# Two four-byte constants in one tile: moving the SBUF tiles of a TensorE-bound kernel by 32 bytes

## The chip, the cores and the metric

The kernel runs on one core of a Trainium2 chip. The metric is the device time of one execution in microseconds. Engines are called TensorE (PE; its weight loads are listed as PEld), VectorE (DVE), ScalarE (ACT), GpSimd (POOL) and SyncE (SP, which issues the DMA transfers here).

## The reference

A two-layer encoder trunk over 256 frames of width 2048, all in float32. Layer 0 mixes in time with an RWKV-7 recurrence of 32 heads, layer 1 with a forgetting attention of 16 heads over shared keys and values. Each is followed by an MLP of width 8192. In short:

```python
x = x + rwkv7_time_mix(rms_norm(x, mix_norm[0]), ...)          # r, k, v projections, decay, gates, recurrence, w_o
x = x + squared_relu_mlp(rms_norm(x, ffn_norm[0]), w_up[0], w_down[0])
k, v, cum_log_f = shared_kv_forget(x, kv_norm, w_kvf, b_f)
x = x + forgetting_attention(rms_norm(x, mix_norm[1]), w_q, w_o, k, v, cum_log_f)
x = x + squared_relu_mlp(rms_norm(x, ffn_norm[1]), w_up[1], w_down[1])
return rms_norm(x, final_norm)

def rms_norm(x, gain):      # RMS_EPS = 1e-6; the recurrence's own norm uses LNX_EPS = 64e-5
    return x * rsqrt(mean(x * x) + RMS_EPS) * gain
def squared_relu_mlp(h, w_up, w_down):
    return square(relu(h @ w_up)) @ w_down
```

## The kernel before

The stream x lies transposed in SBUF, 128 partitions by 16 blocks of 256 frames (`xT`). A projection's weights are streamed from HBM. Each weight and each operand is split into a high part in float32r (fp32r, a float32 that TensorE takes at one column a cycle) and a low part, the rest; a product is the sum of three: high by high, high weight by low operand, low weight by high operand. The operands are kept in two tiles of 32 KB per partition, `opA` and `opB`: for each of the 16 blocks 256 columns of the high part, then 256 of the low.

`load_split` (L192 to L210) fetches a piece of raw weights into `wr`, ScalarE rounds it into `wh` (L204; VectorE at L202 for some), and VectorE or GpSimd takes the rest into `wl` (L206). From there:

- `gemm_steps` (L218) issues three matmuls of 256 columns for each 128x128 block of weights (L212 to L214 in `mm3`). The RWKV stage, the attention's projections and its output use it: 28 groups of 512 output columns in all.
- `gemm_wide` (L240) is the MLP's. For each block of weights it issues one matmul of 512 columns, the high weight over high and low operand together (L254), and one of 256 columns, the low weight over the high operand (L256). This pair is run 4096 times: 64 groups x 16 x 4.
- The values' projection (L933 to L935) turns the roles around: the weights move, 512 columns, over blocks of `opB`. 16 forget-gate columns are projected with `mm3` into `zp`, where the stationary block has 16 columns.
- The gates' projections (L472, L507, L562), the transposes and the attention's own products (L951 to L978) are in plain fp32, each of which is issued as two instructions.

The order of the two streams of the RWKV stage is a table of start and end times (`PLAN_A`, `PLAN_B`); the rest is in program order, with transfers all on SP's queue.

Tiles are laid out in SBUF one after another, each rounded up to 32 bytes per partition. The pool of constants comes first. It begins at byte 16512, a multiple of 64, and holds `vec` (1216 bytes), `k32` (3328), `k16` (1024), `bf` (32), `ones` (512), `eps_r` (32), `eps_l` (32), `negv` (128), `WC` (256) and `onesr` (512), together 7072. The pools of raw and split weights, of the operands, and then of each stage follow from byte 23584. Nearly all larger tiles are multiples of 64 bytes, so that they all lie 32 bytes off a multiple of 64; those behind an odd number of smaller tiles in their own pool (`kk2` and `bk` of the RWKV stage; `qT`, `csb`, `lg`, `pt` and `o` of the attention) lie on one.

`eps_r` is the bias of the norms' logarithm (`Norm.ln`, L326, and L426), `eps_l` that of the recurrence's norm (L819). Each is set by a memset on GpSimd.

Of the kernel before, what the change touches and what calls it, by code (L numbers as in the profile page):

```python
# [10 lines left out]
F32 = mybir.dt.float32  # L11
# [7 lines left out]
P = 128  # L19
# [100 lines left out]
def trunk_kernel(ctx: ExitStack, tc: tile.TileContext, xin, vecs, bfv, c32, c16, w_rkv, w1, w2, a1, a2, g1, g2,  # L120
# [11 lines left out]
    cpool = ctx.enter_context(tc.tile_pool(name="const", bufs=1))  # L132
# [23 lines left out]
    dma(bf, bfv)  # L156
    ones = cpool.tile([P, P], F32, name="ones")
    G.memset(ones, 1.0)
    eps_r = cpool.tile([P, 1], F32, name="eps_r")
    G.memset(eps_r, RMS_EPS)  # L160
    eps_l = cpool.tile([P, 1], F32, name="eps_l")
    G.memset(eps_l, LN_EPS)
    negv = cpool.tile([P, 2 * KT], F32, name="negv")

# [909 lines left out]
def build(nc, arrays):  # L1074
    args = []
    for name, v in arrays.items():
        args.append(nc.dram_tensor(f"in_{name}_dram", v.shape, mybir.dt.from_np(v.dtype), kind="ExternalInput").ap())
    args.append(nc.dram_tensor("out_0_dram", (D, T), F32, kind="ExternalOutput").ap())
    with tile.TileContext(nc) as tc:  # L1079
        trunk_kernel(tc, *args)  # L1080
# [11 lines left out]
```

## Time and profile before

| | before |
|---|---|
| median of 3 runs | 2562.56 us (2562.14, 2562.56 and 2572.66) |
| the profiled execution | 2563.87 us |
| its span, first to last instruction | 2562.1 us |
| TensorE busy | 2474.4 us, 97% |
| VectorE, ScalarE, GpSimd busy | 1620.4, 1272.2, 526.2 us |
| mean granted TensorE clock | 0.993 |
| read from HBM, written | 445.70 MB, 24.13 MB |

The profile is of one execution. Busy times of an engine are unions over its instructions. A matmul's duration overlaps that of the next, because matmuls are pipelined; how fast they follow one another is read from their starts, or from their number in a stretch without idle time. The granted clock (PEclk) of 1.00 is 2.4 GHz, of 0.50 1.2 GHz.

### The profile page before, as it was taken

To read this page: it belongs to the slowest core of one execution; us is meant where nothing else is said; L and a number is where in the kernel's file an instruction comes from. 1 tells how busy PE (TensorE), PEld (TensorE's weight loads), DVE (VectorE), ACT (ScalarE), POOL (GpSimd) and SP (SyncE) were. 2 spreads that over 40 slices of the span, in tenths; PEclk is the share of its full clock that TensorE was granted. 3 is DMA by queue.
4 is the path that set the end of the run, shared out by engine and by line. 5 is a ranking of instruction groups with operands and counts; after the bars stand their busy time and mean duration, and the time that the engine had idled before them with its cause. 6 is when DMAs were issued, how large, how long until landed. Compare 5 with 4: busy or idle time off the path is not lost. (4 is left out here: it accounts for less than half of the span.)

```text
span 2562.1 us, 47095 instructions
## 1 busy us (share of the span) xinstructions
PE 2474.4 (97%) x19102; PEld 2208.3 (86%) x19102; DVE 1620.4 (63%) x2266; ACT 1272.2 (50%) x2098; POOL 526.2 (21%) x428
## 2 busy tenths in 40 slices
PE   6889999999999999999999999999999999999997
PEld 4889988888888888888888898999988888888886
DVE  8987557776755555555556655677555555555555
ACT  3655435454555454454455544455454454554454
POOL 5444324332311211111112100010011112111112
PEclk9999999999999999999999999999999999999998
DMA  4668856555765555555556366546455555556553
GB/s 149 199 201 246 249 180 189 161 166 159 237 202 189 182 181 197 182 189 188 181 181 197 97 183 196 181 158 198 149 190 184 194 187 191 183 195 194 186 195 116
DMA packets 279641, 472.88 MB, mean 185 GB/s; under 512 B 52464, under 2 KB 62976, under 8 KB 279424
## 3 DMA queue, kind: packets, MB, share of 16 engines
q1 hardware_dynamic: 279424, 469.89, 57.9%
q8 instruction: 149, 2.44, 0.4%
q14 instruction: 68, 0.56, 0.1%
HBM read 445.70 MB, written 24.13 MB: 183 GB/s over the span
## 5 line engine op out<-in xcount | busy, mean ns | idle before, releaser
L206 DVE TENSOR_TENSOR wl<-wr,wh 128x1024 fp32r<-128x1024 f32 (+1 forms) x960 | 965.9, 1010 | 740.9 <-ACT wh L204 735.7
L204 ACT CAST wh<-wr 128x1024 fp32r<-128x1024 f32 (+1 forms) x969 | 815.8, 846 | 909.7 <-PE mmw L254 595.0
L254 PE MATMUL mmw<-opB,wh 128*128 128x512 f32 x2048 | 717.4, 397 | 4.9 <-DVE xT L850 4.9
L254 PE MATMUL mmw<-opA,wh 128*128 128x512 f32 x2048 | 718.0, 397 | 0.2 <-ACT wh L204 0.2
L256 PE MATMUL mmw<-opA,wl 128*128 128x256 f32 x2048 | 572.5, 280 | 0.9 <-DVE wl L206 0.9
L256 PE MATMUL mmw<-opB,wl 128*128 128x256 f32 x2048 | 571.7, 279 | 0.0
L254 PEld LDWEIGHTS mmw<-opB,wh 128*128 128x128 f32 x2048 | 384.9, 188 | 97.4 <-DVE xT L850 5.1
L254 PEld LDWEIGHTS mmw<-opA,wh 128*128 128x128 f32 x2048 | 384.9, 188 | 93.0 <-ACT wh L204 0.5
L256 PEld LDWEIGHTS mmw<-opA,wl 128*128 128x128 f32 x2048 | 386.5, 189 | 1.4 <-DVE wl L206 1.3
L256 PEld LDWEIGHTS mmw<-opB,wl 128*128 128x128 f32 x2048 | 386.4, 189 | 0.2
L212 PE MATMUL mm<-opB,wh 128*128 128x256 f32 x1024 | 304.0, 297 | 1.2 <-DVE wh L202 1.2
L214 PE MATMUL mm<-opB,wl 128*128 128x256 f32 x1024 | 294.7, 288 | 7.0 <-DVE wl L206 4.8
L213 PE MATMUL mm<-opB,wh 128*128 128x256 f32 x1024 | 294.6, 288 | 3.9 <-DVE opB L343 3.8
L366 POOL TENSOR_TENSOR xT<-xT,mt 128x512 f32<-128x512 f32 x60 | 128.8, 2147 | 533.8 <-DVE mt L363 533.8
L212 PE MATMUL mm<-opA,wh 128*128 128x256 f32 x768 | 227.7, 297 | 0.0
L214 PE MATMUL mm<-opA,wl 128*128 128x256 f32 x768 | 218.5, 285 | 2.7 <-POOL wl L206 1.5
L213 PE MATMUL mm<-opA,wh 128*128 128x256 f32 x768 | 218.8, 285 | 0.0
L353 POOL TENSOR_TENSOR ms<-mt 128x512 f32<-128x512 f32 x64 | 81.1, 1267 | 636.5 <-ACT mt L351 636.5
L214 PEld LDWEIGHTS mm<-opB,wl 128*128 128x128 f32 x1024 | 198.4, 194 | 9.2 <-DVE wl L206 5.6
L213 PEld LDWEIGHTS mm<-opB,wh 128*128 128x128 f32 x1024 | 198.4, 194 | 7.5 <-DVE opB L343 5.7
L212 PEld LDWEIGHTS mm<-opB,wh 128*128 128x128 f32 x1024 | 198.2, 194 | 5.4 <-DVE wh L202 1.4
L214 PEld LDWEIGHTS mm<-opA,wl 128*128 128x128 f32 x768 | 147.5, 192 | 3.7 <-POOL wl L206 1.7
(252 smaller groups left out, 2711.0 us busy)
## 6 DMA issues: line engine op xcount, KB each, us to landing
wr<-in_mlp_w_up_dram SPq DMA_DIRECT2D x128, 1024.0 KB, 5.4
wr<-in_mlp_w_down_dram SPq DMA_DIRECT2D x128, 1024.0 KB, 5.0
wr<-in_w_rkv_dram SPq DMA_DIRECT2D x96, 512.0 KB, 4.7
wr<-in_w_kvf_dram SPq DMA_DIRECT2D x64, 512.0 KB, 3.7
wr<-in_w_o_dram SPq DMA_DIRECT2D x32, 512.0 KB, 4.0
wr<-in_fox_w_q_dram SPq DMA_DIRECT2D x32, 512.0 KB, 3.8
wr<-in_fox_w_o_dram SPq DMA_DIRECT2D x32, 512.0 KB, 4.0
s_bk<-bk SPq DMA_DIRECT2D x8, 512.0 KB, 3.0
```

Of the source, the lines that this page charges most:

```text
L204: nc.scalar.copy(h, raw[:, k:k + per, :])
L206: (G if share["l"] and c % share["l"] == 0 else V).tensor_tensor(lo, raw[:, k:k + per, :], h.bitcast(F32), op=ALU.subtract)
L212: mm(ps, wh, xh, start=first and bank_first, stop=False, skip_group_check=True)
L213: mm(ps, wh, xl, start=False, stop=False, skip_group_check=True)
L214: mm(ps, wl, xh, start=False, stop=last, skip_group_check=True)
L254: mm(ps[m], h[:, m * P:(m + 1) * P], x[:, k].rearrange("p h t -> p (h t)"), start=k == 0, stop=False, skip_group_check=True)
L256: mm(ps[m][:, 0:T], lo[:, m * P:(m + 1) * P], x[:, k, 0, :], start=False, stop=k == KT - 1, skip_group_check=True)
L353: G.tensor_tensor(s, t, t, op=ALU.mult)
L366: (V if end and g == 3 else G).tensor_tensor(xs, xs, t, op=ALU.add)
```

## The change

The two constants become the two columns of one tile of eight bytes, which is rounded up to 32 bytes as each of them was. What lies behind it in SBUF begins 32 bytes lower: `wr` at 23552 in place of 23584, `opA` at 60416 in place of 60448, and so on. The tiles that lay 32 bytes off a multiple of 64 now lie on one; `kk2`, `bk`, `qT`, `csb`, `lg`, `pt` and `o`, which lay on one, now lie 32 bytes off. `vec`, `k32`, `k16`, `bf` and `ones` stay. The distances between moved tiles stay as they are. Each engine has the same instructions in the same order, and the two memsets are there as before.

```diff
     ones = cpool.tile([P, P], F32, name="ones")
     G.memset(ones, 1.0)
-    eps_r = cpool.tile([P, 1], F32, name="eps_r")
+    eps = cpool.tile([P, 2], F32, name="eps")
+    eps_r, eps_l = eps[:, 0:1], eps[:, 1:2]
     G.memset(eps_r, RMS_EPS)
-    eps_l = cpool.tile([P, 1], F32, name="eps_l")
     G.memset(eps_l, LN_EPS)
     negv = cpool.tile([P, 2 * KT], F32, name="negv")
```

## Rows read from the trace of the kernel before

**Rows 1.** The page: busy us of the engines, and GB/s moved in 40 slices.

```profile
PE 2474.4 (97%) x19102; PEld 2208.3 (86%) x19102; DVE 1620.4 (63%) x2266; ACT 1272.2 (50%) x2098; POOL 526.2 (21%) x428
GB/s 149 199 201 246 249 180 189 161 166 159 237 202 189 182 181 197 182 189 188 181 181 197 97 183 196 181 158 198 149 190 184 194 187 191 183 195 194 186 195 116
```

**Rows 2.** Stretches by stage: from:to, length, busy us (instructions) per engine, clock, DMA.

```profile
36.00:350.00 314.00, 290.05 (x2741) 268.50 (x2739) 244.99 (x376) 167.75 (x332) 137.94 (x120) 0.99 0.70 216
350.00:694.00 344.00, 322.48 (x5127) 289.83 (x5125) 237.78 (x432) 175.10 (x381) 106.31 (x99) 0.99 0.58 174
694.00:1414.00 720.00, 718.44 (x4069) 623.87 (x4070) 424.70 (x469) 349.49 (x475) 118.69 (x71) 1.00 0.58 188
1414.00:1832.00 418.00, 412.16 (x2995) 390.87 (x2994) 267.61 (x497) 210.56 (x408) 29.59 (x40) 1.00 0.54 169
1832.00:2543.00 711.00, 711.00 (x4100) 621.33 (x4099) 407.62 (x445) 349.48 (x467) 114.39 (x69) 1.00 0.57 184
```

**Rows 3.** Waits: who waited for whom, us in total, times, longest.

```profile
ACT wh L204 <- PE mmw L254: 595.0, 359, 1.9
...
ACT wh L204 <- DMA wr<-in_w_rkv_dram: 15.9, 6, 3.8
...
PE hps L425 <- DVE part L424: 11.0, 3, 9.4
PE lps L472 <- POOL xs L451: 10.3, 9, 4.7
...
ACT wh L204 <- DMA wr<-in_mlp_w_up_dram: 2.3, 1, 2.3
```

**Rows 4.** Stretches of PE alone, the MLP of layers 0 and 1.

```profile
726.00:1404.00 678.00, 678.00 (x3838) 1.00 0.58 186
...
1879.00:2521.00 642.00, 642.00 (x3706) 1.00 0.59 190
```

**Rows 5.** Timeline of PE: start us, us; weights of 16 columns, first and 34th.

```profile
1429.15 0.28 PE L212 MATMUL zp<-opB,wh 128*16 128x256 f32 x1
...
1432.89 0.28 PE L212 MATMUL zp<-opB,wh 128*16 128x256 f32 x1
```

**Rows 6.** Timeline of PE: the values' projection, first and 43rd of a run.

```profile
1605.15 0.39 PE L934 MATMUL mmv<-wh,opB 128*128 128x512 f32 x1
...
1614.67 0.39 PE L934 MATMUL mmv<-wh,opB 128*128 128x512 f32 x1
```

**Rows 7.** Timeline of PE: triples of the keys' projection, first and 15th matmul.

```profile
1439.79 0.28 PE L214 MATMUL mm<-opB,wl 128*128 128x256 f32 x1
...
1441.47 0.28 PE L213 MATMUL mm<-opB,wh 128*128 128x256 f32 x1
```

**Rows 8.** Timeline of PE: plain fp32, eight matmuls merged, and the first of them.

```profile
242.19 1.89 PE L507 MATMUL mmg<-gh,wr 128*128 128x256 f32 x8
...
242.19 0.38 PE L507 MATMUL mmg<-gh,wr 128*128 128x256 f32 x1
```

**Rows 9.** Timeline of POOL and ACT: the first memset and the first reader.

```profile
0.88 0.10 POOL L160 MEMSET eps_r<- 128x1 f32 x1
...
15.55 0.47 ACT L426 ACTIVATE gh<-hps,eps_r 128x256 f32<-128x256 f32 x1 [5.04 <-PE hps L425]
```

**Rows 10.** Groups by line and shape: busy us, mean ns, idle before.

```profile
L342 ACT CAST opB<-o 128x256 fp32r<-128x256 f32 x16 | 6.5, 407 | 15.5 <-DVE o L980 15.5
L342 ACT CAST opA<-y 128x256 fp32r<-128x256 f32 x16 | 6.5, 406 | 7.1 <-POOL y L183 6.7
L989 DVE TENSOR_TENSOR qT<-mm,nrq 128x512 f32<-128x512 f32 x8 | 5.4, 683 | 0.0
L916 DVE TENSOR_TENSOR kT<-mm,nr 128x512 f32<-128x512 f32 x8 | 5.1, 682 | 0.0
```

**Rows 11.** Timeline of PE: layer 1's first group, first and 61st matmul of L254.

```profile
1833.06 0.40 PE L254 MATMUL mmw<-opA,wh 128*128 128x512 f32 x1
...
1854.26 0.40 PE L254 MATMUL mmw<-opA,wh 128*128 128x512 f32 x1
```

## The prediction

> **What bounds the kernel now.** I read the busy table first, then the stages, then the steps of TensorE's stream. TensorE (PE) is busy 97% of the span, VectorE (DVE) 63%, ScalarE (ACT) 50% [rows 1]. By stages [rows 2]: both MLP stages (694 to 1414 us and 1832 to 2543 us, 56% of the span) leave PE 1.6 us idle in 1431 us. The attention stage (1414 to 1832) leaves 6, the RWKV stage (36 to 694) 45 in 658. Outside of these lie 36 us of head and 19 of tail. In the MLP the other engines are under 60% busy, and ACT's longest wait there is for PE (595.0 us, for weight buffers to come free), while its waits for weight loads come to 2.3 us for the MLP and 15.9 for the RWKV stage [rows 3]. So the pace at which PE takes one matmul after another sets the time, and whatever doesn't touch that pace is worth a few us.
>
> That pace is above what the columns ask for. I turn each step into cycles at 2.4 GHz, since the granted clock reads 1.00 in the stretches used [rows 4].
> - fp32r, 256 columns, weights of only 16 columns: 33 steps from 1429.15 to 1432.89 us, 113.3 ns = 272 cycles [rows 5]: 16 over the 256 columns.
> - fp32r, 512 columns: 42 steps from 1605.15 to 1614.67 us, 226.7 ns = 544 cycles [rows 6]: 32 over.
> - the usual fp32r triple (L212 to L214), 256 columns and weights of 128: 14 steps from 1439.79 to 1441.47 us, 120.0 ns = 288 cycles [rows 7]: 32 over.
> - the MLP pair (512 and 256 columns, two weight loads): 678 us for 3838 matmuls, 353.3 ns a pair = 848 cycles in layer 0; 642 us for 3706, 346.5 ns = 832 in layer 1 [rows 4]. Over the 768 columns: 80 and 64.
> - plain fp32 (L507), where a column takes two cycles, so that the read runs at half the rate: eight in 1.89 us, each 0.38 long, so 7 steps of 216 ns = 518 cycles for 512 [rows 8]: 6 over.
>
> The excess comes in pieces of 16 cycles per 256 columns, and 16 cycles is the time of 16 columns, 64 bytes per partition. A run of 1024 bytes touches 16 pieces of 64 bytes if it begins on a multiple of 64, and 17 if it begins 32 bytes past one; 17 pieces are 272 cycles. Every fp32r operand here begins 32 past one: the tiles from the raw weights on start at byte 23584 = 368 x 64 + 32. For the 512 columns this needs two reads of 1024 bytes (one of 2048 would be 33 pieces, 528 cycles), so the fit isn't perfect. The fp32 row reads tiles 32 off as well (gh, wr) and shows none of it, as half the rate would leave room to spare. And the weight loads, 512 bytes each (9 pieces for 8), appear as 8 cycles each in layer 1 (832 - 816 = 16 for two) and 16 in layer 0 and in the triples. I take this as the likeliest reading, not as shown: no fp32r operand in this trace lies on a multiple of 64, so nothing separates it from a cost that fp32r always has.
>
> **The change part by part.** *Code:* no instruction is added, removed or moved on any engine. The two memsets on GpSimd (POOL) stay, the first one 0.10 us long at 0.88 us, and their first reader runs at 15.55 us [rows 9], so that the norm's reader now depends on both of them costs nothing; without that lead it would be one memset, 0.10 us.
>
> *Addresses:* everything past the constants moves down by 32 bytes. opA, opB, xT, wr, wh, wl, mt, ms, the inverse's and the recurrence's tiles go from 32 off to a multiple of 64. A few go the other way: kk2, bk, qT, csb, lg, pt and o.
>
> *VectorE, ScalarE:* the same write of 128x512 takes 683 ns into qT (on 64 now) and 682 into kT (32 off); the same cast takes 407 ns from o (on 64) and 406 from y (32 off) [rows 10]. Nothing either way.
>
> *The FoX tiles that go off 64:* their matmuls are fp32 (32 each at L951, L952, L977 and L978, 48 at L972, 176 in all). Bounds: nothing below, one piece of 6.7 ns (113.3 / 17) each above, 1.2 us. I take nothing, since the fp32 row, 32 off, shows no excess.
>
> *Loads:* cheaper or dearer packets would show in the waits for loads. What can be gained is those waits of ACT, 2.3 + 15.9 us, were all of them to go; what can be lost isn't bounded by them, but ACT and DVE have the idle time quoted. I take nothing.
>
> *PE's stream,* the term that decides. If the extra piece goes, a read is bound by its columns and the 6 cycles of the fp32 row: 272 becomes 262 (10 saved), 544 becomes 518 (26 saved). For a weight load I take off 8 cycles, the smaller of the two excesses seen; the bounds are 0 and all of it.
> - MLP: 26 + 10 + 2 x 8 = 52 cycles a pair, 21.7 ns, by 4096 pairs: 88.7 us. Layer 1's pair would be at its floor, 518 + 262 = 780. Both stages have no cover: PE waits for nobody. At 6% more pace DVE goes from 59% to 63% busy and loads from 188 to 200 GB/s, where the trace has slices of 246 and 249 [rows 1].
> - triples of the attention stage: 12 groups x 16 x 4 x 3 = 2304 matmuls by 18 cycles, 7.5 ns: 17.3 us.
> - triples of the RWKV stage: the other 3072 (of 5376), 23.0 us; there DVE is busy 78% from 36 to 350 us [rows 2] and PE's longest waits are for DVE and POOL [rows 3], so I count half, 11.5 us.
> - L933 to L935: 384 by 26 cycles, 10.8 ns: 4.2 us.
>
> Sum 121.7 us. The profiled execution took 2563.87 us (span 2562.1), 1.3 over the median of 2562.56. 2563.9 - 121.7 = 2442. With nothing off the weight loads: 4096 x 15.0 = 61.4, triples 10 cycles, 9.6 + 6.4, and 4.2: 81.6, so 2482. With all of it: layer 0 and its 1984 steady pairs 68 cycles, 56.2 us, the other 2112 pairs 45.8, triples 26 cycles, 25.0 + 33.3 with the RWKV stage in full, and 4.2: 164.5, so 2399.
>
> **The rivals.**
> *No change.* The 16 cycles per 256 columns are what fp32r costs at full rate, wherever the operand lies. For it: no row shows an aligned fp32r read, the 512-column row needs the split above, and the pace is a steady one, equal in opA and opB. Against it: the excess is a whole piece of 64 bytes, twice. The time is then that of before, 2562, but for the step between 848 and 832 cycles. It is a state: layer 0's window holds the slow one for 678 us; layer 1's first group has it too, 60 pairs from 1833.06 to 1854.26 us, 353.3 ns each [rows 11]; and from 1879 us on it is quick [rows 4], with the same instructions in all three. If layer 0 came into the quick state, 1984 x 6.8 ns = 13.5 us would go: 2549 to 2550, the edge of what can be told from no change.
> The Trainium skill ("SBUF — State Buffer", Specifications (TRN2)) gives SBUF cachelines of 16 bytes. By that a tile 32 bytes off a multiple of 64 begins on a line as much as one that isn't, and this rival's 2562 would be the time; no run here shows the size of a line, and the pieces of 64 bytes above speak against 16 being all there is.
>
> *Slower.* Layer 1 falls into the state of layer 0: its two reads meet as they do there, each load costs 16 cycles and not 8. 1984 pairs x 6.8 ns = 13.5 us: 2577. It decides at the hand-over after the first group of layer 1, around 1856 us, where the norm's matmuls interrupt the stream. For it: the state follows from small differences of timing, and one of the three runs of before took 2572.66, 10 us more than the others. Against it: two runs and the profile agree within 1.8 us.
>
> *The change doesn't do what it says.* The addresses are in the built program, so this is out for the tiles; for the time it is the first rival.
>
> **How the numbers follow.** The piece goes: 0.42, between 2399 and 2482, forecast 2442. It goes in part (weights alone, or moving operands of one size alone), 2482 to 2549: 0.10. No change within 0.5%, about what a measurement of this kernel can tell from none: 0.36. Slower by over 0.5%: 0.12, most of it the state in layer 1, the rest the loads. Faster is 0.42 + 0.10 = 0.52. The range must reach from the first case to the no-change case: 2405 to 2575; it leaves out some 0.04 below and 0.12 above. The forecast's own range is 2399 to 2482.
>
> **What would show it.** Right: the window of each MLP layer holds pairs of about 325 to 335 ns, the 512-column rows 216 ns, the 16-column rows 109 ns, the triples 110 to 113 ns, and fp32 rows still 216. Moving operands alone: the 512 rows fall and the triples stay above 115. Wrong: 113.3, 226.7 and 120.0 ns stand unmoved; then the excess belongs to fp32r. If the steps fall and the time falls less, the RWKV stage shows the lost part as PE idle time ended by DVE. If only the MLP windows move, and by 6.8 ns a pair, it is the state and not the change.

## The result, and the profile after

The kernel after the change takes 2573.48 us (median of 18 runs, 2571.02 to 2577.61), the kernel before in the same comparison 2562.97 (18 runs, 2550.33 to 2582.09). The ratio is 1.0037, 95% interval 1.0021 to 1.0053: a loss of 10.5 us between the medians (9.5 by the ratio), where 2442 us was forecast. The profiled execution took 2574.62 us, its span 2572.8.

The steps on which the forecast rested, from the timeline of PE of the kernel after (start us, duration us). The first two rows are 33 matmuls apart, the next two 42, the next two 18, and the last row is eight plain fp32 matmuls merged:

```profile
1429.84 0.28 PE L213 MATMUL zp<-opB,wh 128*16 128x256 f32 x1
...
1433.58 0.28 PE L213 MATMUL zp<-opB,wh 128*16 128x256 f32 x1
...
1576.37 0.39 PE L935 MATMUL mmv<-wl,opB 128*128 128x512 f32 x1
...
1585.89 0.39 PE L935 MATMUL mmv<-wl,opB 128*128 128x512 f32 x1
...
1439.75 0.28 PE L212 MATMUL mm<-opB,wh 128*128 128x256 f32 x1
...
1441.91 0.28 PE L212 MATMUL mm<-opB,wh 128*128 128x256 f32 x1
...
241.69 1.89 PE L507 MATMUL mmg<-gh,wr 128*128 128x256 f32 x8
```

3.74 us / 33 = 113.3 ns, 9.52 / 42 = 226.7, 2.16 / 18 = 120.0, and 1.89 us for the eight: the figures of [rows 5 to 8] to the last digit. The operands now begin on a multiple of 64 bytes and none of these steps moved.

What moved is the MLP of layer 1. Stretches of PE in the kernel after (from:to, length, busy us (instructions), clock, DMA), the same two as [rows 4]:

```profile
726.00:1404.00 678.00, 678.00 (x3837) 1.00 0.58 186
1879.00:2521.00 642.00, 642.00 (x3636) 1.00 0.58 186
```

Layer 0 has 3837 matmuls in its 678 us, as before (3838), 353.3 ns a pair. Layer 1 has 3636 in place of 3706: 642 / 1818 = 353.1 ns a pair in place of 346.5. The busy table of the page agrees, PE alone being longer than in [rows 1]:

```profile
PE 2487.1 (97%) x19102; PEld 2215.7 (86%) x19102; DVE 1621.8 (63%) x2266; ACT 1272.1 (49%) x2098; POOL 526.4 (20%) x428
```

The stages as the starts of the MLP's first L254 and last L256 in each layer bound them (us, from the timelines of the two profiles):

| | to the first pair | MLP, layer 0 | attention | MLP, layer 1 |
|---|---|---|---|---|
| before | 694.4 | 734.2 | 403.7 | 711.4 |
| after | 695.3 | 734.3 | 401.4 | 724.6 |

Layer 1 is 13.2 us longer. It parts from the kernel before at one point, the interruption by the norm's matmuls, here in the timelines of PE of before and of after:

```profile
1854.96 1.02 PE L324 MATMUL nps<-nacc,ones 128*128 128x256 f32 x4
```

```profile
1853.60 1.03 PE L324 MATMUL nps<-nacc,ones 128*128 128x256 f32 x4
```

In both kernels the first group of layer 1 ahead of it steps at 353.3 ns. Behind it every group of the kernel before steps at 346.7 and every group of the kernel after at 353.3, with the same instructions and the same interruption of some 1 us. In layer 0 the same interruption takes both kernels from 346.7, the step of the first group, to 353.3. In the last group of layer 0 both go back to 346.7 behind waits of 0.17 and 0.95 us for split weights, so that 346.7 does occur in the kernel after too, though not behind the norm's matmuls.

### The profile page after: what moved, and what is told of

Read it like the earlier page. It is cut to its first block, busy times and chain, and to the rows that moved or that the text cites. A ratio compares the mean times of both kernels' runs of the same rounds, so it can differ in the third digit from the quotient of the medians.

```text
span 2572.8 us, 47095 instructions
## 1 busy us (share of the span) xinstructions
PE 2487.1 (97%) x19102; PEld 2215.7 (86%) x19102; DVE 1621.8 (63%) x2266; ACT 1272.1 (49%) x2098; POOL 526.4 (20%) x428
## 5 line engine op out<-in xcount | busy, mean ns | idle before, releaser
L254 PE MATMUL mmw<-opB,wh 128*128 128x512 f32 x2048 | 724.2, 399 | 5.3 <-DVE xT L850 5.3
L254 PE MATMUL mmw<-opA,wh 128*128 128x512 f32 x2048 | 724.4, 399 | 0.2 <-ACT wh L204 0.2
L256 PE MATMUL mmw<-opA,wl 128*128 128x256 f32 x2048 | 576.3, 281 | 0.9 <-DVE wl L206 0.9
L256 PE MATMUL mmw<-opB,wl 128*128 128x256 f32 x2048 | 575.6, 281 | 0.0
L254 PEld LDWEIGHTS mmw<-opB,wh 128*128 128x128 f32 x2048 | 385.5, 188 | 100.8 <-DVE xT L850 5.5
L254 PEld LDWEIGHTS mmw<-opA,wh 128*128 128x128 f32 x2048 | 385.5, 188 | 95.8 <-ACT wh L204 0.5
L256 PEld LDWEIGHTS mmw<-opA,wl 128*128 128x128 f32 x2048 | 387.8, 189 | 1.5 <-DVE wl L206 1.4
L256 PEld LDWEIGHTS mmw<-opB,wl 128*128 128x128 f32 x2048 | 387.8, 189 | 0.2
```

The source lines that it names most:

```text
L254: mm(ps[m], h[:, m * P:(m + 1) * P], x[:, k].rearrange("p h t -> p (h t)"), start=k == 0, stop=False, skip_group_check=True)
L256: mm(ps[m][:, 0:T], lo[:, m * P:(m + 1) * P], x[:, k, 0, :], start=False, stop=k == KT - 1, skip_group_check=True)
```

## Experiments

Terms: the *distance* of an operation is the start of its moving operand less the start of its weights, in bytes modulo 256. In before and after it is 0 for pairs and triples alike. *Quick* is a group of the MLP (64 pairs) at 346.7 ns (832 cycles), *slow* one at 353.3 (848). Theory at the outset: the steps belong to fp32r (the no-change rival), and a state of the MLP's stream, picked at the interruption, makes the loss; rival: the start of the operands matters after all.

**The steps by themselves (`m1_steps`).** Streams of matmuls only, with moving operand and weights at chosen places past a multiple of 64 bytes; nothing of the reference is computed.

```diff
+CONF = [("trip", 0, 0), ("trip", 8, 8), ("trip", 0, 8), ("trip", 8, 0), ("trip", 4, 4), ("wide", 0, 0), ...]
+mm(b, W[:, 0, w:w + P], X[:, c:c + 512], ...)      # "wide": c and w begin 0, 4 or 8 floats past the multiple
```

> This kernel computes nothing of the reference: it is a stream of matmuls alone, in short segments with one plain fp32 matmul of 8 to 187 columns ahead of each, and writes one product to the output. Segments differ in the type and columns of the moving operand and in where the operands begin past a multiple of 1024 bytes (z = 0, q = 16, h = 32 bytes; first letter the moving operand, second the weights). Theory (fp32r costs 17 cycles for 16 columns wherever its operand lies; the rest is a state of the weight loads): 512 columns at 226.7 ns and 256 columns over 16-column weights at 113.3 ns for every start; 256 columns over 128-column weights near 120 ns for every start; bfloat16 of 512 columns near 216 ns; MLP pairs at 346.7 or 353.3 ns, both values within each of the four placements, chosen anew by the matmul ahead of a segment and with shares that don't differ between the placements. Rival (the start decides the state): the pairs with both operands on a multiple of 64 are nearly all at 353.3, those with both 32 bytes off at both values. Second rival (the distance of the operands decides): the placements with one operand shifted differ from the two with both.

Timeline of PE, 24 matmuls merged to a row (start us, us). In a name the first letter is the moving operand's place, the second that of the weights: z on the multiple, h 32 bytes past it. `wide` is 512 columns, `slim` 256 columns on weights of 16, `trip` 256 on weights of 128, `bwid` 512 in bfloat16:

```profile
25.65 3.03 PE L131 MATMUL triphhx<-X,W 128*128 128x256 f32 x24
...
31.36 2.96 PE L131 MATMUL triphzx<-X,W 128*128 128x256 f32 x24
...
36.99 5.66 PE L133 MATMUL widezzx<-X,W 128*128 128x512 f32 x24
42.49 5.63 PE L133 MATMUL widehhx<-X,W 128*128 128x512 f32 x24
...
53.51 2.90 PE L135 MATMUL slimzzx<-X,W 128*16 128x256 f32 x24
56.24 2.90 PE L135 MATMUL slimhhx<-X,W 128*16 128x256 f32 x24
58.98 5.35 PE L137 MATMUL bwidzzx<-XB,WB 128*128 128x512 bf16 x24
64.17 5.34 PE L137 MATMUL bwidhhx<-XB,WB 128*128 128x512 bf16 x24
```

zz and hh take the same time: 226.6 to 227.9 ns a step for 512 columns, 113.3 to 113.8 for 13 of the 16 slim ones, 119.6 to 120.0 for triples. Bfloat16 takes 215.8 (518 cycles) and, for 256 columns, 109.2 (262), at either place. So the excess is fp32r's own, 17 cycles for 16 columns, and the start on 32 or 64 is nothing. With both operands 16 bytes past the multiple, 512 columns took 229.9 to 233.4 ns, so at 16 the start does count for a little. Two things were not expected. Where moving operand and weights lie at *different* places, the step moves: triples 116.5 to 117.8 ns for hz. And the pairs came in both states at a common place (9 of 24 segments quick at zz, 19 of 24 at hh, where the expectation of `m2_scan` has 18), but in 24 of 24 quick at hz. In this run and in both scans below, the small matmuls meant for the first 52 segments ran in one block ahead of all of them, so those segments follow each other without one.

**Is it the multiple of 64? (`pad32`, `pad64`).** The changed kernel with everything behind the norm's constants moved up again, by 32 (the addresses of before) or by 64 bytes (a multiple of 64 again).

```diff
     G.memset(eps_l, LN_EPS)
+    cpool.tile([P, 8], F32, name="pad")        # pad64: 16
```

> The changed kernel with 32 bytes of unused space behind the shared tile, so that every later tile lies where it lay before the change. If the place of the tiles makes the difference: as the kernel before, a ratio of 1.000 with the spread of before (2550 to 2582 us), against 1.0037 for the change. If the shared tile itself does it (its two writers, its reader's dependence): as the change, 2573 us with little spread.

> The changed kernel with 64 bytes of unused space behind the shared tile: tiles lie on multiples of 64 as after the change, but 64 bytes past the multiples of 1024 on which they lie there. If being on a multiple of 64 makes the difference: 2573 us with little spread, a ratio of 1.004. If it is the multiple of 1024, or nothing but which state a build happens to fall into: some other value between 2550 and 2582, 1.000 or the spread of before.

`pad32`: 2563.16 us, ratio to before 1.0001 (0.9979 to 1.0022). `pad64`: 2566.36, ratio 1.0012 (0.9992 to 1.0032). `pad64` lies on multiples of 64 as the changed kernel does and shows at most a part of its loss. In the profile of each, layer 0 is quick and layer 1 slow, the reverse of before; stretches of PE in `pad32`:

```profile
726.00:1380.00 654.00, 654.00 (x3772) 1.00 0.58 189
1880.00:2480.00 600.00, 600.00 (x3398) 1.00 0.58 186
```

654 / 1886 = 346.8 ns and 600 / 1699 = 353.1. `pad32` has the addresses of before, so there each layer can fall either way, which fits most of the spread of before's times (2550 to 2582): 2 x 13 us between both layers quick and none. The kernel after, 2571 to 2578 in 18 runs, fits both slow in every run.

**The scan of distances (`m2_scan`, `m3_scan`).** Streams alone again, the moving operand 0 to 1008 bytes behind the weights in steps of 16 (pairs), then the kernel's triples and pairs at 0 to 240.

```diff
+        for i in range(16):
+            seg("trip", 4 * i, 0, 16)          # moving operand 16 * i bytes past the weights' place
+            if rep < 8:
+                seg("pair", 4 * i, 0, 16)
```

> As m1_steps this kernel computes nothing of the reference, only streams of matmuls in short segments with one fp32 matmul ahead of each. First part: the weights begin on a multiple of 1024 bytes, the moving operand 0 to 1008 bytes past one in steps of 16, MLP pairs three times and triples twice each. Second part: both operands 0, 32, 64, 96, 128, 256 and 512 bytes past a multiple of 1024, MLP pairs 24 times each. Theory (the distance between the operands decides what a weight load costs, their common place nothing): in the first part the step depends on the distance and repeats with some period, 346.7 and 116.6 ns at 32 bytes; in the second part every place has both states with the same shares. Rival (the common place decides the shares): in the second part 0 has few quick segments (9 of 24 in m1_steps) and 32 many (18 of 24), and 64, 128, 256 and 512 go with 0.

> As m2_scan it computes nothing of the reference: streams of the triples as the kernel issues them (high weights over high and low operand, low weights over the high operand) and of MLP pairs, with the moving operands 0 to 240 bytes past the weights in steps of 16, 12 and 8 segments each, and both operands 32, 64 and 96 bytes past a multiple of 1024. Theory (distance decides): triples of 350 ns at 32 bytes in every segment, 360 at 0; pairs of 346.7 at 32, 144 and 160 and of 353 at 64, 112 and 192; if best96 is right, triples of about 340 at 192.

Ten triples of `m3_scan` at distance 0, then ten at 112, timeline of PE (30 matmuls apart: 3.60 us, 360.0 ns a triple, and 3.40 us, 340.0):

```profile
955.74 0.28 PE L133 MATMUL tripaaaax<-X,W 128*128 128x256 f32 x1
...
959.34 0.28 PE L133 MATMUL tripaaaax<-X,W 128*128 128x256 f32 x1
...
1038.11 0.28 PE L133 MATMUL tripahaax<-X,W 128*128 128x256 f32 x1
...
1041.51 0.28 PE L133 MATMUL tripahaax<-X,W 128*128 128x256 f32 x1
```

The pattern repeats every 256 bytes, so one period stands for all. Step in ns, pairs from both scans, triples (three matmuls) from the second; where segments fall on several values, these are named:

| distance | 0 | 16 | 32 | 48 | 64 | 96 | 112 | 128 | 144 | 160 | 192 | 224 |
|---|---|---|---|---|---|---|---|---|---|---|---|---|
| pair | 346.7 or 353.3 | 346.7, rarely 360.0 | 346.7 | 350, some 346.7 | 349 or 354 | 350 | 353.3 | 351 | 346 to 348 | 346.7 | 353.3 | 353.3, rarely 346.7 |
| triple | 360 | 340, 350 or 356 | 350 | 355 | 353, once 340 | 360 | 340 | 356 or 360 | 350 or 356 | 352 or 356 | 340 or 353 | 355 |

At the steps of 226.7 and 113.3 ns the columns would take 544 + 272 = 816 cycles, 340.0 ns, for the pair, and three times 272, also 340.0, for the triple. What is above I put down to the weight loads, since 256 columns take 113.3 ns with weights of 16 columns: none for the triple at 112, 16 cycles a load at 0; mostly 8 to 16 a load for the pair. At a common place the share of quick segments was 12 of 26, 20 of 24 and 7 of 24 (0, 32, 64) in one scan and 4 and 6 of 12 (32, 64) in the other, so the place alone doesn't pick the state. The tile `fx` of the small matmuls lies a multiple of 256 bytes from the place of distance 0, so each of these places also has one distance to `fx`; that distance alone doesn't pick the state either.

**In the kernel (`ops32`, `wts32`).** The operands moved 32 bytes up against their weights (in the kernel after), and 32 down (in the kernel before); all else at its place.

```diff
+    big.tile([P, 8], F32, name="padlo")        # wts32: 248
     opA = big.tile([P, KT, 2, T], F32R, name="opA")
...
+    big.tile([P, 248], F32, name="padhi")      # wts32: 8
```

> The changed kernel with unused space ahead of opA and behind xT, so that opA, opB and xT lie 32 bytes past a multiple of 1024 and the weights and all other tiles on one. Theory (distance decides): the MLP pairs are at 346.7 ns in both layers in every run and the triples near 117 ns in place of 120: 2550 (the fastest runs of before, both layers quick) less 2304 x 3.4 ns = 8 us and some of 3072 x 3.4 = 10 us: 2535 to 2545, a ratio near 0.991, and little spread. Rival (state by chance): 2550 to 2577 as before, triples at 120.

> The kernel before with unused space that puts opA, opB and xT on a multiple of 1024 and leaves the weights 32 bytes past one, the reverse of ops32. Theory (distance decides): pairs mostly at 352.7 to 353.3 ns (19 of 24 segments in m1_steps) and triples at 118.2: 2577 less about 4 to 10 us, 2566 to 2573. Rival (state by chance): the spread of before around 2563.

`ops32`: 2540.56 us, ratio 0.9943 (0.9919 to 0.9967), pairs 346.7 in both layers, triples 350.0. `wts32`: 2569.28, ratio 1.0049 (1.0026 to 1.0073), pairs 353.3 in both layers of its profile. The sign of the distance counts, as in the scan (32 and 224). These two kernels alone don't show it: `ones`, the tile of ones that the norm's matmuls read, lies 64 past the operands in `ops32` and 96 in `wts32`, and the next experiments show that this counts too.

**What picks the state at a common place? (`draw_before`, `draw_after`).** A small plain fp32 matmul of `ones` by `ones`, like the norm's, ahead of each of the 64 groups, in a length that differs from group to group; its result is overwritten.

```diff
+        n = 8 + wide["n"] * 37 % 120
+        mm(ps[0][:, 0:n], ones, ones[:, 0:n], start=True, stop=True, skip_group_check=True)
         for k0 in range(0, KT, WK):
```

> The kernel before with one small plain fp32 matmul (8 to 127 columns) ahead of each of the 64 groups of the MLPs, into a bank that the group then overwrites, so that the state of the pairs is drawn anew 64 times in a run. It costs some 64 x 0.1 to 0.2 us. Theory (the phase at which a stream of pairs starts picks the state; 32 bytes off a multiple of 64 it is mostly the quick one, 39 of 48 segments in m2_scan): some 75 to 85% of the groups at 346.7 ns a pair. Rival (place says nothing, only the hand-over does): half of the groups in both of this kernel and draw_after.

> The same with the changed kernel. Theory: tiles on a multiple of 1024 have fewer quick groups, 35 to 50% (12 of 26 segments at 0 in m2_scan, 9 of 24 in m1_steps), so this is slower than draw_before by some 64 groups x 0.35 x 64 pairs x 6.7 ns = 10 us. If the slow state of the changed kernel were fixed by the place alone: all 64 groups at 353.3. Rival (place says nothing): the same time as draw_before within 3 us.

In the kernel before 53 of 64 groups are quick, in the kernel after 2. Stretches of PE in `draw_before` (those of `draw_after` stand below; a draw each 23 us is among the counts):

```profile
726.00:1380.00 654.00, 654.00 (x3778) 1.00 0.58 187
1880.00:2480.00 600.00, 600.00 (x3482) 1.00 0.58 189
```

Ratios 1.0031 (1.0004 to 1.0059) and 1.0102 (1.0056 to 1.0148). So the two layouts differ nearly each time such a matmul interrupts the stream, and it isn't a draw with even chances. Of what this matmul reads, the change moved only the distance of `ones` (not moved) to the stream's tiles (moved): it was 64 bytes past the operands' place before and is 96 now, modulo 256 (64 in `pad32`, 32 in `pad64`).

**Is it `ones`? (`draw_shift`, `draw_ones`, `swap_ones`).** `draw_shift`: `draw_before` with all tiles 32 bytes higher, `ones` too (a padding of 8 floats ahead of `vec`). `draw_ones` and `swap_ones`: the changed kernel with and without the draws, with `ones` laid ahead of `bf`, 32 bytes lower, so that its distance is 64 again while operands and weights stay on multiples of 64; the 32 bytes of `bf` move behind it, and nothing else moves.

```diff
+    ones = cpool.tile([P, P], F32, name="ones")
     bf = cpool.tile([HEADS, 1], F32, name="bf")
     dma(bf, bfv)
-    ones = cpool.tile([P, P], F32, name="ones")
     G.memset(ones, 1.0)
```

> draw_before with 32 bytes of unused space ahead of all constants, so that every tile, ones among them, moves up by 32 bytes: the operands lie on a multiple of 64, and every distance between tiles is that of the kernel before. Theory (the distance of ones, which the fp32 matmul ahead of a stream reads and which the change left where it was, to the stream's tiles picks the state): most of the 64 groups quick, as in draw_before (some 55), 2562 to 2572 us. Rival (the common place picks it): nearly none quick, as in draw_after (2 of 64), 2578 to 2588 us.

> draw_after with the tiles ones and bf in the other order, which moves ones down by 32 bytes and nothing else: the operands stay on a multiple of 1024, and ones is as far from them as before the change. Theory (distance of ones): most of the 64 groups quick, 2562 to 2572 us. Rival (common place): nearly none, 2578 to 2588 us.

> The changed kernel with ones and bf in the other order, no draws added. Theory (distance of ones): as the kernel before, some 2560 us with its spread from 2546 to 2580. Rival (common place): as the change, 2571 to 2578 us with little spread.

`draw_shift` and `draw_ones` have 53 quick groups each, and the other eleven are the same eleven as in `draw_before`, so something that differs from group to group, such as the length of the draw, counts too. Ratios 1.0025 (0.9997 to 1.0054) and 1.0025 (0.9996 to 1.0054). Stretches of PE, `draw_after`, then `draw_ones` (a draw each 23 us is among the counts):

```profile
726.00:1380.00 654.00, 654.00 (x3725) 1.00 0.57 185
1880.00:2480.00 600.00, 600.00 (x3417) 1.00 0.57 184
```

```profile
726.00:1380.00 654.00, 654.00 (x3778) 1.00 0.58 187
1880.00:2480.00 600.00, 600.00 (x3483) 1.00 0.58 189
```

`swap_ones` takes 2555.29 us (2541.67 to 2561.66, 12 runs), ratio 0.9979 (0.9953 to 1.0005): the changed kernel without its loss. In its profile the layers stand as before's again, slow and quick:

```profile
726.00:1380.00 654.00, 654.00 (x3702) 1.00 0.57 187
1880.00:2480.00 600.00, 600.00 (x3464) 1.00 0.59 190
```

**Better distances (`best96`, `best112`, `best144`).** Paddings that give pairs and triples each a distance of their own: 32 and 192 in `best96`, 16 and 112 in `best112`, 144 and 112 in `best144`. For the last two the operands begin 16 bytes inside a larger tile.

```diff
+    big.tile([P, 48], F32, name="padlo")       # best112, best144: 24
     opA = big.tile([P, KT, 2, T], F32R, name="opA")
...
+    big.tile([P, 56], F32, name="padhi")       # best144: 32
...
+    cpool.tile([P, 24], F32, name="pad")       # best112: 40, best144: 8
```

> ops32 with the weights of the triples (the pools of wr, wh and wl outside the MLPs) moved to 96 bytes past a multiple of 256, so that their operand lies 192 bytes further modulo 256, where single matmuls of 256 columns ran at 113.3 ns in 7 of 8 segments of m2_scan; the MLP's tiles are as in ops32. If the triples follow the single matmuls: 340 to 343 ns a triple in place of 350 in ops32, 2304 / 3 x 8 ns = 6 us in the attention stage and some of as much in the RWKV stage, 2530 to 2535. If the second matmul of a triple, whose operand is the low part, meets its load elsewhere: no gain, 2540, or a loss.

> The operands 16 bytes past the MLP's weights and 112 past the triples' weights modulo 256, the distances at which m3_scan had pairs of 346.7 ns in 8 of 8 segments and triples of 340 to 342.5 in 12 of 12. By those: pairs 346.7 in all groups, triples 341.5 in place of 360, 18.5 ns x 768 = 14 us in the attention stage and up to 19 us in the RWKV stage, so 2550 less 14 less some 7 to 10: 2526 to 2530, with little spread.

> The operands of the products (both halves of opA and opB) lie 144 bytes past a multiple of 256, the MLP's weights on one, the triples' weights 32 past one. So the pair's moving operand stands 144 bytes behind its weights and the triple's 112. Theory (the distance modulo 256 bytes sets what a weight load costs): pairs 346.7 ns in all 64 groups, as in all segments of both scans at 144, and triples about 341 as in best112, where the pairs alone went wrong: MLP stages as in best96, triples another 4 to 10 ns lower than there in part of the groups, so 2526 to 2533 us, 0.990 or below of the kernel before. Rival (the state is picked at the hand-over by another tile's distance, which the scans' streams have only in part): a third of the pairs or more at 353.3 or 360.0 ns, as in best112, and a time above 2545.

`best96`: 2533.91 us, ratio 0.9900 (0.9869 to 0.9931); pairs 346.7 in all groups, but for short waits in the last two of layer 0. Triples of the keys' projection, timeline of PE, 15 matmuls apart, 1.70 us = 113.3 ns each where [rows 7] have 120.0:

```profile
1449.76 0.28 PE L216 MATMUL mm<-opB,wh 128*128 128x256 f32 x1
...
1451.46 0.28 PE L216 MATMUL mm<-opB,wh 128*128 128x256 f32 x1
```

`best112` missed: 2584.24 us, ratio 1.0087 (1.0055 to 1.0118). Its triples came as forecast, 340.0 to 345 ns, but nearly all groups of pairs ran in a third state, 360.0 ns (864 cycles, 24 a load), which one segment of three at 16 had shown in `m2_scan` and which I had passed over. Stretches of PE:

```profile
726.00:1380.00 654.00, 654.00 (x3635) 1.00 0.56 182
1880.00:2480.00 600.00, 600.00 (x3336) 1.00 0.57 183
```

`best144`: 2538.20 us, ratio 0.9892 (0.9853 to 0.9931), triples 340 to 347, and all groups quick but for some 60 pairs: the second half of the next to last group of layer 0 and the first half of the last, behind a short wait, ran at 353.3. So 144 has a second state too, which no segment of the scans had shown. The steps are otherwise as expected, the absolute time is 5 us above the 2533 that I gave as the upper end; it ran beside a kernel before of 2561.88, so by the ratio it stands level with `best96`.

**Which distance of `ones`? (`b112_ones64`, `b112_ones80`, `b144_ones240`).** `best112` and `best144` with `ones` alone at another place. In `best112` `ones` lies 80 past the operands and 96 past the weights and the norm's sums.

```diff
+    ones = cpool.tile([P, P + 8], F32, name="ones")[:, 4:4 + P]      # b112_ones80, against best112
+    G.memset(ones, 1.0)
     bf = cpool.tile([HEADS, 1], F32, name="bf")
     dma(bf, bfv)
-    ones = cpool.tile([P, P], F32, name="ones")
-    G.memset(ones, 1.0)
...
-    cpool.tile([P, 40], F32, name="pad")
+    cpool.tile([P, 32], F32, name="pad")
```

> best112 with `ones` 32 bytes lower (64 past a multiple of 256 in place of 96), as in swap_ones; nothing else moves. Theory (the norm's matmuls at the hand-over pick the state): the distance of `ones` to the norm's squares `ms` and to the MLP's weights is 64 again, as in the kernel before, and if that distance is the one that matters, most groups leave 360.0 for 346.7 ns and the time falls from 2584 to 2535 or below (ratio about 0.991). Rival (360.0 belongs to a distance of 16 bytes between operands and weights, whatever `ones` does): nearly all groups at 360.0 as in best112, a ratio of about 1.009.

> best112 with `ones` at 80 past a multiple of 256: its distance to the operands is 64, as in the kernel before, that to `ms` and to the MLP's weights 80. If the distance of `ones` to the operands is the one that matters, most groups go to 346.7 ns and the ratio to about 0.991; if it is that to `ms` or the weights, this kernel differs from b112_ones64; if neither, nearly all groups stay at 360.0 and the ratio at about 1.009.

> best144 with `ones` at 240 past a multiple of 256, 96 from the operands, which is the distance that was slow where operands and weights lie at a common place; operands, weights and `ms` stay. Theory (at a distance of 144 there is one state alone, so nothing at the hand-over can pick another): pairs 346.7 in all groups, 2534 to 2544 us, ratio 0.987 to 0.993. Rival (best144 was quick by the place of `ones`): 353 or 360 ns in a large part of the groups and a ratio above 0.995.

`b112_ones80`, where `ones` lies 64 past the operands (80 past weights and sums): 2538.99 us, ratio 0.9933 (0.9907 to 0.9959), all groups quick. One of its nine executions took 6126.43 us, for no reason that the record shows, and isn't in the ratio; the other eight took 2530.66 to 2544.60 (median 2538.38). Stretches of PE:

```profile
726.00:1380.00 654.00, 654.00 (x3771) 1.00 0.58 189
1880.00:2480.00 600.00, 600.00 (x3464) 1.00 0.59 190
```

`b112_ones64`, 64 past the weights and sums and 48 past the operands: 2584.28, ratio 1.0123 (1.0077 to 1.0168), layer 0 quick and layer 1 at 360.0 in its profile, which is of the fastest of its four runs (2568.16 to 2589.72):

```profile
726.00:1380.00 654.00, 654.00 (x3773) 1.00 0.58 189
1880.00:2480.00 600.00, 600.00 (x3335) 1.00 0.57 183
```

So a distance of 64 to the *operands* of the stream went with quick groups, as in the kernel before, and one of 64 to the weights didn't. That points to the operands; it isn't shown, since the 80 to weights and sums in `b112_ones80` could be a quick place of its own. `b144_ones240` puts it at 96 from the operands, the slow place of the changed kernel: 2533.47, ratio 0.9916 (0.9887 to 0.9945), all groups quick but for the second half of layer 0's last, at 353.3 behind its wait:

```profile
726.00:1380.00 654.00, 654.00 (x3774) 1.00 0.59 190
1880.00:2480.00 600.00, 600.00 (x3463) 1.00 0.59 189
```

So at 144 the norm's matmuls led to the quick state with `ones` at 208 (`best144`) and at 96 from the operands. At 32 only one place of `ones` was tried: it is 64 from the operands in `ops32` and in `best96`.

## Why the prediction was wrong

*What bounds the kernel:* right. PE's pace sets the time; each pair slower in layer 1 came out in full, 13.2 us longer in that stage. The profiled execution is only 10.75 us longer, mainly since its attention stage was 2.3 us shorter.

*Code, memsets, loads, VectorE, ScalarE, the FoX tiles:* right, nothing that shows. Groups by line and shape of the kernel after, the same as [rows 10], with `o` and `y`, `qT` and `kT` having changed places on 64:

```profile
L342 ACT CAST opB<-o 128x256 fp32r<-128x256 f32 x16 | 6.5, 407 | 15.4 <-DVE o L980 15.4
L342 ACT CAST opA<-y 128x256 fp32r<-128x256 f32 x16 | 6.5, 406 | 6.4 <-POOL y L183 6.0
...
L989 DVE TENSOR_TENSOR qT<-mm,nrq 128x512 f32<-128x512 f32 x8 | 5.4, 684 | 0.0
L916 DVE TENSOR_TENSOR kT<-mm,nr 128x512 f32<-128x512 f32 x8 | 5.1, 683 | 0.0
```

*PE's stream:* the step that failed, all of its 121.7 us. I read 16 cycles over 256 columns as one piece of 64 bytes too many, from operands that begin 32 bytes off. The equality of 16 cycles with 64 bytes fitted in number alone: the trace couldn't test it, as the prediction itself said, and the 512-column row already needed an assumption of its own. The kernel after and `m1_steps` show the same 113.3, 226.7 and 120.0 ns on the multiple, and `m1_steps` 518 and 262 cycles for bfloat16 at either place. What I called the floor (518 + 262) holds for bfloat16 and plain fp32 and not for fp32r. A chance of 0.52 for faster was far too much for a reading with no row on its other side. That 2573 lies inside the range of 2405 to 2575 is luck: its upper end was drawn from the case of no change.

*The weight loads:* I took them for the same piece. By the scans they are a cost of their own, 0 to 24 cycles a load, which goes by the distance of operand and weights modulo 256 bytes, and, where that distance has several states, by what interrupted the stream. The change keeps that distance at 0, so it had nothing to gain from it, and the state of layer 1 to lose.

*No change* was right about every step, and its 2562 is nearer than the forecast. By the Trainium skill ("SBUF — State Buffer", Specifications (TRN2)), with its cachelines of 16 bytes, 32 bytes off would make no difference. The steps of `m1_steps` at 0 and 32 agree with that (226.6 to 227.9 ns); those at 16, also the start of such a line, don't (229.9 to 233.4).

*Slower* is what happened, by its mechanism (layer 1 in the state of layer 0), at its place (the hand-over) and nearly at its price: 13.5 us forecast, 13.2 measured in the stage, 10.5 between the medians, which fits if layer 1 of the kernel before is slow too in some of its runs. What it got wrong is the condition. I put the state down to small differences of timing and so gave it 0.12; it hangs on the distance between `ones`, which the change leaves, and the tiles that it moves (`draw_shift`, `draw_ones`, `swap_ones`): with operands and weights at distance 0, an interruption by `ones` at 96 led to the slow state nearly each time, at 64 to either, to the quick one more often. The prediction noted that the distances between *moved* tiles stay and never looked at those between moved and unmoved ones.

*Open.* Why the load of a weight block costs more at some distances, why the state lasts from one interruption to the next, and what in the meeting of `ones` and the operands picks it: the runs show that it is so, not through what. Whether the distance of `ones` to the operands or to another moved tile counts is open too. The two scans disagree on the share of quick segments at a common place, and so at the same distance to `fx` (20 of 24 and 4 of 12 at 32), so something ahead of the interruption must count as well.

## What to carry to other kernels

A surplus that fits a mechanism in whole numbers isn't evidence until a row without the suspected cause shows it gone; where none is in the trace, a microkernel of a few matmuls settles it, and until then no change is the likelier case. Shifting tiles changes their distance to every tile that stays, so list what the interrupting operations read as well as what the main stream reads. Where TensorE's pace is the bound and fp32r is used, try the distance of moving operand and weights modulo 256 bytes: 32 bytes for pairs and 192 for triples here bring 1.0% over the kernel before for three paddings.

## What was not expected of the hardware

- fp32r costs 17 cycles for 16 columns in the places tried on a multiple of 32: 113.3 ns for 256 columns, 226.7 for 512; bfloat16 109.2 and 215.8. The Trainium skill ("TensorE: Matmul & The Clock Gate", Back-to-back issue gap) gives 262 and 518 cycles as the gap of isolated matmuls of 256 and 512 columns, and some 131 ns for 512 in a stream with weight loads; the streams of bfloat16 here, with a load for each matmul, agree with the 262 and 518 (109.2 and 215.8 ns) and not with the 131.
- A weight load that lies behind a running fp32r matmul isn't free: 256 columns took 113.3 ns with weights of 16 columns and 120.0 with 128 in one layout, and by the distance 113.3 to 120.0 with the same 128. The Trainium skill ("TensorE: Matmul & The Clock Gate", Step-by-step: what each phase is for) has two independent read ports for the two, so that a load takes no read bandwidth from the running matmul. For fp32r the step grows with the load at most distances all the same; whether through the ports isn't shown.
- One stream of the same instructions can run at 346.7 or 353.3 ns a pair at distance 0 and at 346.7 or 360.0 at 16 (8, 16 or 24 cycles a load). In the profile of the kernel before it changed from one to the other only behind the norm's matmuls, a wait or another stage.
- The norm's sum, 1 us of plain fp32 matmuls, can cost 13 us in the 711 behind it by where its tile `ones` lies.
